# A diffusion backbone layer on one core: the vs projection by seven block products, stages reordered

## The chip, the cores and the metric

The kernel runs on one core of one Trainium2 chip. The metric is the device time of one execution in microseconds, lower is better. TensorE (PE) multiplies matrices, VectorE (DVE) and ScalarE (ACT) work elementwise, GpSimd (POOL) and SyncE (SP) here mainly issue DMAs; ACT issues a few as well.

## The reference

One layer with 512 latent tokens of width 1024 and 256 context tokens, all in float32. After a modulated RMS norm the input `hx` goes through one wide projection, and its parts feed two branches:

```python
z = h @ w_in
u, vs, q, r, ga, gb, k, v, lr = _split(z, IN_SPLITS)
a = _spatial_gating(gelu(u), gelu(vs), ...)     # u * (w_s . layer_norm(vs) + b_s), per chunk of 128 tokens
o, s_f, s_b = _gla_bidir(qh, k, v, lr, ...)      # gated linear attention, 4 heads, both directions
o = o * rsqrt(mean(o * o) + EPS)                 # per head
ob = o * gla_norm_g * silu(r)
merged = sigmoid(ga) * (a @ w_br_a) + sigmoid(gb) * (ob @ w_br_b)
x = x + g1x * (merged @ w_o)
```

Then a convolutional feed-forward (`ffn_w_up`, a 3x3 depthwise convolution, `ffn_w_down`) is added in the same way, and a final RMS norm gives the output. u, vs, r, ga and gb are each a product of 512 x 1024 by 1024 x 1024. The modulation vectors come from `c` through `w_ada`.

## The kernel before

**Float32 by three matmuls.** Every operand is split into a rounded high part and the residual, and a product is the sum of three matmuls (high x high, high x residual, residual x high) with 512 columns. A weight block of 512 KB (two or eight slices of 128 rows, 1024 numbers per partition) is loaded by SP (`stream_load`, line 237), cast by ACT (`wh`, line 249) and its residual made by DVE (`wl`, line 250). Five buffers each hold raw blocks, high parts and residuals. `specs` is the list of all blocks in the order of use; `weights()` takes the next one.

**Stages**, in order: first head's q, k, v; the other heads' k and q (`x_unit`), v of the last two heads (`v_units`); vs (`wide_tm`: four token tiles by two column halves, each 24 matmuls of line 408); u (eight units of 24 matmuls of line 390, channels first); r, ga, gb and the product with `w_br_a` (`gate`); the products with `w_br_b` and `w_o` (`wide_tm`); the feed-forward.

**Seven block products.** `gate` cuts a 1024 x 1024 product into two by two quadrants on either side and multiplies seven combinations instead of eight quadrants (the Strassen-Winograd scheme). Each of the seven has 24 matmuls (line 1360) and two weight blocks. The sums of quadrants of the input are made once (`hx_sum`, from a copy of `hx` in HBM, `fx_kept`). The sums of quadrants of the weights are made in HBM by POOL's DMAs: for each of two blocks of rows four copies, then four accumulating copies (`sums_build`, lines 214 and 216). A step of this is taken at each `weights()` call and at every second hook, and waits for the last matmul before it in the program; `SUMS0` and `DENSE` say where they start and where two are taken at once. For each gate ACT copies finished banks (`taken`) and DVE combines them (`combine`, line 1348).

**Hooks.** The attention of a head is a list of steps (transposes, scores, start state, states, decay of the next head, output); a hook between matmuls takes one step from the list. Before, the hooks in vs hold the third and fourth heads' attention. u's loop holds `sgu_part` (line 1252 and the two DVE instructions at 1254 and 1256), one unit late, which multiplies the normalised vs by the spatial weights and then by u; the result is written to HBM by POOL (`kept`). r's output goes through Silu and is multiplied by the attention output (`r_gate`); `ob_turn` (line 1336) transposes it and writes it to HBM during ga and gb.

**Background.** `ada2` builds the later modulation vectors on DVE (line 1216, one 256 KB load each), in steps called ticks: the list `ticks` says how many at each block of the gates. `behind_last` and `in_order` fix the order of such instructions on their engine. Otherwise a planner orders each engine's instructions when the program is built, by priority and its own costs. Two pools of 2 KB tiles, `heap` (43) and `late` (26), hold nearly everything; PSUM has four banks `mm` and four `gl`.

Of the kernel before, what the change touches and what calls it, by code (L numbers as in the profile page):

```python
# [16 lines left out]
P = 128  # L17
# [15 lines left out]
ENDS = 4  # L33
LEAD = 5
EARLY = 8
SUMS0 = 84
ADA2 = 7
DENSE = 10
SHSC = 6
# [5 lines left out]
def backbone_kernel(  # L45
# [27 lines left out]
    def late(shape, dt=F32, s="l"):  # L73
        return lp.tile(shape, dt, tag="l", name=nm(s))
# [69 lines left out]
    def w_cols(w, c0, n=P, k0=0, kn=KT):  # L144
        specs.append((w[k0 * P:(k0 + kn) * P, c0:c0 + n].rearrange("(k p) c -> p k c", p=P), kn, n))

    wi = w_in[0]
    for h in range(1, NH):
# [2 lines left out]
                w_cols(wi, O_V + 512, 512, 2 * k, 2)  # L151
        w_cols(wi, O_K + h * P)
        w_cols(wi, O_Q + h * P)
    for hf in range(2):
        for k in range(KT // 2):
            w_cols(wi, O_VS + hf * 512, 512, 2 * k, 2)
    for j in range(KT):
        w_cols(wi, O_U + j * P)
    R_AT = len(specs)
# [7 lines left out]
    def quarters(w, c0):  # L167
        return lambda b, row, col: w[(4 * b + 2 * row) * P:(4 * b + 2 * row + 2) * P,
                                     c0 + col * 512:c0 + (col + 1) * 512]

    def sum_tiles(blocks):
        return [[dp.tile([2 * P, 576], F32, name=nm("sum"))[:, :512] for _ in range(4)] for _ in range(blocks)]
# [6 lines left out]
        return ffn_w_down[0][r0:r0 + HALF[b] * P, col * 512:(col + 1) * 512]  # L179

    sums = [[dp.tile([n * P, 576], F32, name=nm("sum"))[:, :512] for _ in range(4)] for n in HALF]
    gate_weights = [(quarters(wi, c0), sum_tiles(2)) for c0 in (O_R, O_GA, O_GB)]
    gate_weights.append((quarters(w_br_a[0], 0), sum_tiles(2)))
    down_specs, specs = specs, []
    for g_quarter, g_sums in gate_weights:
# [81 lines left out]
    def weights():  # L267
        i = pos[2]
        pos[2] += 1
        for at, steps_ in building:  # L270
            for _ in range((i >= at) + (at <= i < DENSE)):
                next(steps_, None)
        stream_split(i + 2)
        stream_load(i + 1 + AHEAD)
        return splits.pop(i)
# [744 lines left out]

    def hook():
        hooked[0] += 1
        if hooked[0] % 2 and pos[2] < R_AT:
            next(building[1][1], None)
        if hooks:
            f = hooks.pop(0)
            f[0](*f[1:])
# [86 lines left out]
    o_tiles(1)  # L1114
    hooks += steps(1)
    v_units()
    ctx_k(3, x_unit(kxs, 3))
    x_unit(qxs, 3)
    o_tiles(2)
    hooks += steps(2)  # L1120
    o_tiles(3)
    hooks += steps(3)

# [2 lines left out]
    V.tensor_copy(ones_r, ones)  # L1126
    sw, swT, sgb = [], [], []

    def sgu_load():
        for i in range(2):  # L1130
            sw.append(late([P, 4, P], s="sw"))
            dma(sw[i], sgu_w[0, 4 * i:4 * i + 4].rearrange("g p q -> p g q"))
        for i in range(2):
            sgb.append(heap([P, 4, P], s="sgb"))
            dma(sgb[i], sgu_b[0:1, 4 * i:4 * i + 4, :].rearrange("o g p -> o (g p)").to_broadcast([P, 512]))

    def sgu_turn(i):
        ps = gl()
# [19 lines left out]
    vraw = [[None] * 4 for _ in range(2)]  # L1158
    stats = const([P, 4, 2, 6], "stats")

    behind = []

    def vs_done(hf, t, ps):
        vraw[hf][t] = (late if hf else heap)([P, 512], s="vr")
        A.activation(vraw[hf][t], ps, AF.Gelu)

        for h_, t_ in ((), ((), ((0, 0), (0, 1), (1, 0), (1, 1)), ((0, 2), (0, 3), (1, 2)), ((1, 3),))[t])[hf]:
            V.bn_stats(stats[:, t_, h_, :], vraw[h_][t_])
        if hf and t == 0:
            sgu_load()  # L1170
            behind.append(len(traced()))
        if hf and t == 1:
            in_order(behind.pop(), V.engine)

    wide_tm(hx, vs_done, hook)
    while hooks:
        hook()
    mv = const([P, 4, 2], "mv")
    for t in range(4):
        V.bn_aggr(mv[:, t, :], stats[:, t, :, :])  # L1180
    var = const([P, 5, 4], "var")
    V.tensor_scalar(var[:, 1:5, :], oss, 1.0 / 256, None, op0=ALU.mult)
    V.tensor_copy(var[:, 0, :], mv[:, :, 1])
    A.activation(var, var, AF.Sqrt, bias=eps_t, scale=1.0)
    V.reciprocal(var, var)
    vrs, ors = var[:, 0, :], var[:, 1:5, :]
    for hf in range(2):
        for t in range(4):
            z = vraw[hf][t]
            V.tensor_scalar(z, z, mv[:, t, 0:1], vrs[:, t:t + 1], op0=ALU.subtract, op1=ALU.mult)  # L1190


    bc_g = {}
# [45 lines left out]
                V.reduce_sum(cols[kind][:, j * 4:j * 4 + 4], t_, axis=AX.X)  # L1239
            yield  # L1240

    a_kept, ob_kept = [], {}
# [6 lines left out]
    def sgu_part(j, ug):  # L1249
        ps = gl()  # L1250
        for t in range(4):
            T.matmul(ps[:, t * P:(t + 1) * P], vraw[j // 4][t][:, (j % 4) * P:(j % 4 + 1) * P], swT[j // 4][:, j % 4, :], start=True, stop=True)  # L1252
        s_ = heap([P, 4, P], s="sg")
        V.scalar_tensor_tensor(s_, ps.rearrange("p (t r) -> p t r", t=4), lng[:, j:j + 1],
                               sgb[j // 4][:, j % 4, :].unsqueeze(1).to_broadcast([P, 4, P]), op0=ALU.mult, op1=ALU.add)
        V.tensor_tensor(ug, s_.rearrange("p t r -> p (t r)"), ug, op=ALU.mult)
        a_kept.append(spill(ug))

    hx_sums = {}

    def hx_sum(b):
        def quad(i, hf):
            t_ = heap([P, 2, 256], s="fq")
            for kk in range(2):
                dma(t_[:, kk], fx_kept[4 * b + 2 * i + kk][:, hf * 256:(hf + 1) * 256])
            return t_

        def kept(name, t_, p, q, op):
# [6 lines left out]
        a21, a22, a11, a12 = quad(0, 1), quad(1, 1), quad(0, 0), quad(1, 0)  # L1275
        kept("p1", a22, a21, a22, ALU.subtract)
        yield
        kept("s3", a21, a11, a21, ALU.subtract)
        yield
        kept("s2", a11, a22, a11, ALU.subtract)  # L1280
        yield
        kept("q4", a12, a12, a11, ALU.add)
        yield

    pieces = [z for z in (hx_sum(0), hx_sum(1)) for _ in range(4)]

    prev = None
    for j in range(KT):
        if j:
            next(pieces[j - 1])  # L1290
        w = weights()
        ps = mm()
        prod_cm(ps, w, hx)
        ug = heap([P, S], s="ug")
        A.activation(ug, ps, AF.Gelu)
        if j < 2:
            for i in range(2):
                (sgu_turn, sgu_bias)[j](i)
        if prev is not None:
            sgu_part(*prev)  # L1300
        prev = (j, ug)
    next(pieces[-1])
    sgu_part(*prev)


    ob_t = {}
# [10 lines left out]
    r_sum = of_sums(lambda name, b: hx_sums[name, b])  # L1317

    def r_silu(src):
        z = late([P, 512], s="obt")  # L1320
# [41 lines left out]

    banks = []

    def gate(out, pool, at={}, mids=late, quad=r_quad, sum_=r_sum):
# [24 lines left out]
        for t in range(2):  # L1390
            out(1, t + 2, combine(m5[t], X[t], ALU.subtract, pool))
        later(4)
        gate_product(Z, sum_("q4"))
        for t in range(2):
            out(1, t, combine(Z[t], u2[t], ALU.subtract, pool))
        later(5)
        gate_product(X, quad("a22"))
        later(6)
        for t in range(2):
            out(0, t + 2, X[t])  # L1400

    pending = []

    def r_out(hf, t, src):
# [3 lines left out]
        else:  # L1408
            pending.append((hf, t, z))

    bg += [ada2("g1"), ada2("sh", "sc", ahead=SHSC)]
    ticks = [0] * 2 + [1] * 6 + [0] * 6 + [0, 0] + [1] * 12 + [0, 1] * 7 + [1, 1, 2] * 5
    gate(r_out, heap, mids=heap)

    def squash(dst, name):
        def out(hf, t, src):
# [21 lines left out]

    sga, sgb_t = {}, {}
    def ga_step(i):  # L1440
        if i < 4:
            r_gate(*pending.pop(2 if i < 2 else 0))
        if i > 1:
            ob_turn(i - 2)

    gate(squash(sga, "sga"), heap, {i: lambda i=i: ga_step(i) for i in range(7)}, heap)
    found = {}

    def a_prep():
# [448 lines left out]
```

## Time and profile before

| | |
|---|---|
| median of 3 runs | 908.09 us (907.87 to 908.47) |
| profiled execution, span | 906.9 us |
| its own time, with what lies around the span as at the median | 906.9 + 1.2 = 908.1 us |
| PE busy | 892.4 us (98%), 4464 matmuls |
| DVE busy | 719.3 us (79%) |
| ACT busy | 468.7 us (52%) |
| POOL busy | 98.6 us (11%) |
| moved by DMA | 202.41 MB, mean 223 GB/s |
| queue of SP and ACT / queue of POOL | 137.39 MB, 47.1% / 61.04 MB, 30.4% of 16 engines |

The profile is of one execution. Times in it count from the span's start. L390 is line 390 of the kernel; in a group `mm<-hxh,wh` the tile written stands before the arrow. After the bar stand the busy time, the mean of one instruction in ns, and the idle time of the engine just before with what ended it. A matmul's own duration (390 ns) is longer than the distance from one to the next, as they are pipelined. A DMA share above 1 is possible, since it adds up the time of packets of several queues.

### The profile page before, as it was taken

The numbers are of one execution on the slowest core, as the hardware profiler recorded it, in microseconds if no ns is written. First come the engines' busy times: TensorE is split into PE (matmuls) and PEld (weight loads), VectorE is DVE, ScalarE is ACT, GpSimd is POOL, SyncE is SP. The second block draws the span as 40 slices with busy tenths as digits, with TensorE's granted clock in tenths as the row PEclk, the third lists the DMA queues.
The fourth block names the chain that finished last, engine by engine and source line by source line (L and its number), as shares of the span: only waits on it lengthen the run. The fifth ranks groups of instructions, "written<-read, shape, count | busy, mean of one in ns | idle before, by whom it ended". The sixth has DMA issues, their size and how long they took to land.

```text
span 906.9 us, 12500 instructions
## 1 busy us (share of the span) xinstructions
PE 892.4 (98%) x4464; PEld 744.0 (82%) x4464; DVE 719.3 (79%) x1205; ACT 468.7 (52%) x778; POOL 98.6 (11%) x154
## 2 busy tenths in 40 slices
PE   7999999999999999999999999999999999999996
PEld 5778888888888888888888889888888888888885
DVE  6468687869786478688998868897899987896996
ACT  6256455747533557678531448433343434356763
POOL 1311231212112200000000010001111110000000
PEclk9999999999999999999999999999999999999998
DMA  9985996899979999886999651998998893256552
GB/s 278 346 275 158 265 272 120 170 315 156 241 254 245 245 294 330 262 282 190 361 367 350 202 169 38 287 299 180 191 218 179 175 196 96 89 167 207 174 183 96
DMA packets 157291, 202.41 MB, mean 223 GB/s; under 512 B 9465, under 2 KB 88645, under 8 KB 157229
## 3 DMA queue, kind: packets, MB, share of 16 engines
q1 hardware_dynamic: 131229, 137.39, 47.1%
q0 software_dynamic: 24160, 61.04, 30.4%
q10 hardware_dynamic: 1840, 3.18, 0.9%
q8 instruction: 35, 0.57, 0.3%
q14 instruction: 27, 0.22, 0.1%
HBM read 193.19 MB, written 65.01 MB: 285 GB/s over the span
## 4 chain that ended last, share of the span: by engine, by line
PE 95%; DVE 1%; ACT 1%; DMA 1%; SPq 0%; issue 0%; ACTq 0%
PE mm L390 33%; PE mm L408 15%; PE mm L1360 12%; PE gl L1795 10%; PE gl L1360 5%; PE gl L926 3%; PE mm L690 2%; PE gl L408 2%; PE mm L1795 2%; PE gl L690 1%; PE mm L1038 1%; PE mm L1088 1%; PE gl L599 1%; PE gl L961 1%; PE gl L1252 1%; DMA wa<-in_w_ada_dram 1%
## 5 line engine op out<-in xcount | busy, mean ns | idle before, releaser
L249 ACT CAST wh<-raw 128x1024 fp32r<-128x1024 f32 x183 | 189.0, 1036 | 201.3 <-PE mm L390 104.0
L250 DVE TENSOR_TENSOR wl<-raw,wh 128x1024 fp32r<-128x1024 f32 x183 | 218.3, 1199 | 71.6 <-ACT wh L249 63.0
L390 PE MATMUL mm<-h2h,wh 128*128 128x512 f32 (+1 forms) x344 | 133.0, 387 | 0.0
L390 PE MATMUL mm<-h2l,wh 128*128 128x512 f32 (+1 forms) x344 | 133.0, 387 | 0.0
L390 PE MATMUL mm<-h2h,wl 128*128 128x512 f32 (+1 forms) x344 | 133.0, 387 | 0.0
L1647 DVE SCALAR_TENSOR_TENSOR cacc<-ca,ccol,cacc 128x441 f32<-128x441 f32 (+2 forms) x176 | 121.8, 694 | 4.4
L390 PEld LDWEIGHTS mm<-h2h,wl 128*128 128x128 f32 x344 | 64.6, 188 | 13.2
L390 PEld LDWEIGHTS mm<-h2l,wh 128*128 128x128 f32 x344 | 64.6, 188 | 13.1
L390 PEld LDWEIGHTS mm<-h2h,wh 128*128 128x128 f32 x344 | 64.6, 188 | 13.0
L1795 PE MATMUL gl<-wh,dah 128*128 128x512 f32 x132 | 51.3, 389 | 0.0
L1795 PE MATMUL gl<-wl,dah 128*128 128x512 f32 x132 | 51.3, 389 | 0.0
L1795 PE MATMUL gl<-wh,dal 128*128 128x512 f32 x132 | 51.3, 389 | 0.0
L1216 DVE SCALAR_TENSOR_TENSOR acc<-wa,cs,acc 128x512 f32<-128x512 f32 x64 | 45.8, 744 | 0.0
L1648 ACT ACTIVATE cacc<-cacc 128x512 f32<-128x512 f32 x22 | 13.9, 633 | 59.2 <-DVE cacc L1647 59.1
L214 POOL DMA_DIRECT2D sum<-in_ffn_w_down_dram x24 | 13.2, 554 | 281.6 <-PE mm L408 184.5
L390 PE MATMUL mm<-hxh,wh 128*128 128x512 f32 x104 | 41.3, 397 | 0.0
L390 PE MATMUL mm<-hxl,wh 128*128 128x512 f32 x104 | 40.6, 390 | 0.0
L390 PE MATMUL mm<-hxh,wl 128*128 128x512 f32 x104 | 40.5, 390 | 0.0
L216 POOL DMA_DIRECT2D sum<-sum x28 | 25.2, 899 | 113.1 <-PE mm L390 49.6
L408 PE MATMUL mm<-wh,hxh 128*128 128x512 f32 x88 | 34.7, 395 | 0.0
L408 PE MATMUL mm<-wl,hxh 128*128 128x512 f32 x88 | 34.4, 391 | 0.0
L408 PE MATMUL mm<-wh,hxl 128*128 128x512 f32 x88 | 34.3, 390 | 0.0
(464 smaller groups left out, 2031.4 us busy)
## 6 DMA issues: line engine op xcount, KB each, us to landing
raw<-sum SPq DMA_DIRECT2D x52, 512.0 KB, 4.4
wa<-in_w_ada_dram SPq DMA_DIRECT2D x96, 256.0 KB, 6.2
raw<-in_w_in_dram SPq DMA_DIRECT2D x46, 512.0 KB, 5.8
raw<-in_ffn_w_up_dram SPq DMA_DIRECT2D x44, 512.0 KB, 5.5
sum<-in_w_in_dram POOLq DMA_DIRECT2D x36, 512.0 KB, 7.7
sum<-in_ffn_w_down_dram POOLq DMA_DIRECT2D x30, 512.0 KB, 6.5
sum<-sum POOLq DMA_DIRECT2D x26, 512.0 KB, 7.4
raw<-in_ffn_w_down_dram SPq DMA_DIRECT2D x15, 512.0 KB, 4.2
```

The costliest lines, as they stand in the source:

```text
L216: G.dma_start(sums[b][dst], ap, accum_op=ALU.add)
L249: A.copy(wh, raw)
L250: V.tensor_tensor(wl, raw, wh.bitcast(F32), op=ALU.subtract)
L390: T.matmul(ps, a[:, k, :], b[:, c0:c0 + n], start=(k == 0 and i == 0), stop=(k == KT - 1 and i == 2))
L408: T.matmul(ps, a[:, t * P:(t + 1) * P], b[:, k % 2, :], start=(k == 0 and i == 0), stop=(k == KT - 1 and i == 2))
L690: T.matmul(fps[i], a, b, start=(k == 0 and z == 0), stop=(k == KT - 1 and z == 2))
L926: T.matmul(ps, p_, q_, start=(start and z == 0), stop=(stop and z == 2))
L1216: behind_last(lambda: V.scalar_tensor_tensor(acc[i], coming.pop(0), cs[:, k, 0:1], acc[i], op0=ALU.mult, op1=ALU.add), V)
L1360: T.matmul(banks[t], a(kk, t), w[:, kk, :], start=(first and b == 0 and kk == 0 and i == 0), stop=(b == 1 and kk == 1 and i == 2), skip_gr ...
L1647: V.scalar_tensor_tensor(o, a_[:, r0 + dy:r1 + dy, c0 + dx:c1 + dx], wcol(tap), o, op0=ALU.mult, op1=ALU.add)
L1648: A.activation(acc, acc, AF.Gelu)
L1795: T.matmul(ps, a, w[:, kk, :], start=(first and kk == 0 and i == 0), stop=(last and kk == n_ - 1 and i == 2), skip_group_check=True)
```

## The change

- The order becomes u, r, vs, ga, gb. vs goes through `gate` and has its own quadrant sums in HBM, so `specs` has 14 blocks for vs behind r in place of 8 ahead of u, and `SUMS0` moves from 84 to 90. Five gates' sums (80 steps) are built in place of four (64).
- Sum steps are taken at every hook from the eighth block on, and from r on at two of three blocks.
- The third head's attention is put on the hook list ahead of k and q of the fourth; the rest of it and the fourth head's runs in u, with two hooks in each unit.
- u's Gelu is taken later than its matmuls (up to three units wait in PSUM), the results stay in SBUF until ga.
- `hx_sum` is spread over u and the first two products of r; the last sum ("q4") is written over the upper-right quadrant of `hx`, which no gate reads.
- r's outputs are multiplied by the attention in r and vs, `ob_turn` runs in vs and ga, the spatial weights are loaded in r and turned in vs, and `sgu_part` runs in ga, two after each of four products, with its results written to HBM on ACT's queue.
- The ticks are spread anew: five in r, seven in vs, as before from ga on.

```diff
-SUMS0 = 84
+SUMS0 = 90
...
-    for hf in range(2):
-        for k in range(KT // 2):
-            w_cols(wi, O_VS + hf * 512, 512, 2 * k, 2)
...
-    gate_weights = [(quarters(wi, c0), sum_tiles(2)) for c0 in (O_R, O_GA, O_GB)]
+    gate_weights = [(quarters(wi, c0), sum_tiles(2)) for c0 in (O_R, O_VS, O_GA, O_GB)]
...
-            for _ in range((i >= at) + (at <= i < DENSE)):
+            for _ in range((i >= at and not (at == 1 and i >= R_AT and i % 3 == 0)) + (at <= i < DENSE)):
                 next(steps_, None)
...
-        if hooked[0] % 2 and pos[2] < R_AT:
+        if (hooked[0] % 2 or pos[2] >= 8) and pos[2] < R_AT:
             next(building[1][1], None)
...
     v_units()
+    o_tiles(2)
+    hooks += steps(2)
     ctx_k(3, x_unit(kxs, 3))
     x_unit(qxs, 3)
-    o_tiles(2)
-    hooks += steps(2)
     o_tiles(3)
     hooks += steps(3)
...
-    wide_tm(hx, vs_done, hook)
-    while hooks:
-        hook()
...
-        a_kept.append(spill(ug))
+        spills.append((j, ug))
...
     for j in range(KT):
-        if j:
-            next(pieces[j - 1])
         w = weights()
-        ps = mm()
-        prod_cm(ps, w, hx)
...
+        ups.append(mm())
+        for k in range(KT):
+            prod_k(ups[-1], w, hx, k, 0, S)
+            if k == 3:
+                hook()
+                for _ in range((0, 0, 1, 1, 1, 2, 1, 1)[j]):
+                    u_out()
+        hook()
+        if j == 2:
+            piece()
+        if j == 7:
+            piece()
+    u_out()
+    while hooks:
+        hook()
+    piece()
...
+    def r_step(i):
+        if i < 2:
+            piece()
+        if i in (3, 5):
+            sgu_load(i // 2 - 1)
+
+    bg += [ada2("g1", ahead=5), ada2("sh", "sc", ahead=SHSC)]
+    ticks = [0] * 4 + [1, 0] * 5 + [1, 0] * 7 + [0, 0] + [1] * 12 + [0, 1] * 7 + [1, 1, 2] * 5
+    gate(r_out, heap, {i: lambda i=i: r_step(i) for i in range(7)}, heap)
...
+    def vs_out(hf, t, src):
+        z = vraw[hf][t] = heap([P, 512], s="vr") if not hf else src
+        A.activation(z, src, AF.Gelu)
+        V.bn_stats(stats[:, t, hf, :], z)
+
+    def vs_step(i):
+        if i < 4:
+            r_gate(*pending.pop(2 if i < 2 else 0))
+        if i in (1, 2):
+            sgu_turn(i - 1)
+        if i in (3, 5):
+            sgu_bias(i // 2 - 1)
+        if i > 0:
+            ob_turn(i - 1)
...
+    gate(vs_out, heap, {i: lambda i=i: vs_step(i) for i in range(7)}, late, pool1=late)
...
+    def sgu_step(i):
+        while spills:
+            j, ug = spills.pop(0)
+            a_kept[j] = spill(ug, adma)
+        for n in ((), (0, 1), (2, 3), (4, 5), (6, 7), (), ())[i]:
+            sgu_part(SGU_ORDER[n])
...
     def ga_step(i):
-        if i < 4:
-            r_gate(*pending.pop(2 if i < 2 else 0))
-        if i > 1:
-            ob_turn(i - 2)
+        if i < 2:
+            ob_turn(i + 6)
+        sgu_step(i)
...
     def gb_step(i):
-        if i < 3:
-            ob_turn(i + 5)
         a_step((4, 2, 2, 2, 2, 2, 2)[i])
```

More of the change, by code (lines that the diff above doesn't have):

```diff
@@ L1127, in backbone_kernel, with sgu_load @@
     sw, swT, sgb = [], [], []
[L1129 to L1135, printed above, removed]
+    def sgu_load(i):
+        sw.append(late([P, 4, P], s="sw"))
+        dma(sw[i], sgu_w[0, 4 * i:4 * i + 4].rearrange("g p q -> p g q"))
+        sgb.append(heap([P, 4, P], s="sgb"))
+        dma(sgb[i], sgu_b[0:1, 4 * i:4 * i + 4, :].rearrange("o g p -> o (g p)").to_broadcast([P, 512]))
     def sgu_turn(i):
@@ L1154, in sgu_bias @@
                                    lnb[:, 4 * i + g:4 * i + g + 1], sgb[i][:, g, :], op0=ALU.mult, op1=ALU.add)
[L1158 to L1173, printed above, removed]
-    wide_tm(hx, vs_done, hook)
-    while hooks:
-        hook()
[L1178 to L1190, printed above, removed]
     bc_g = {}
@@ L1240, in ada2 @@
             yield
-    a_kept, ob_kept = [], {}
+    a_kept, ob_kept = {}, {}
     def spill(src, start=G.dma_start):
@@ L1247, in spill, with sgu_part @@
         return d
-    def sgu_part(j, ug):
+    ugs, spills = [], []
+    def sgu_part(j):
+        ug = ugs[j]
         ps = gl()
@@ L1273, in kept @@
             hx_sums[name, b] = pair
-        a21, a22, a11, a12 = quad(0, 1), quad(1, 1), quad(0, 0), quad(1, 0)
+        a21, a22, a11 = quad(0, 1), quad(1, 1), quad(0, 0)
+        yield
         kept("p1", a22, a21, a22, ALU.subtract)
+        yield
+        kept("s2", a22, a22, a11, ALU.subtract)
+        a12 = quad(1, 0)
         yield
@@ L1279, in hx_sum, with piece, u_out @@
         yield
-        kept("s2", a11, a22, a11, ALU.subtract)
-        yield
[L1282 to L1287, printed above, removed]
+        V.tensor_tensor(a12, a12, a22, op=ALU.add)
+        for kk in range(2):
+            hi, lo = (z[:, 256:512] for z in hx[4 * b + kk])
+            A.copy(hi, a12[:, kk])
+            V.tensor_tensor(lo, a12[:, kk], hi.bitcast(F32), op=ALU.subtract)
+        yield
+    sums_of = [hx_sum(0), hx_sum(1)]
+    def piece():
+        behind_last(lambda: [next(z) for z in sums_of], V)
+    ups = []
+    def u_out():
+        ug = heap([P, S], s="ug")
+        A.activation(ug, ups.pop(0), AF.Gelu)
+        ugs.append(ug)
     for j in range(KT):
-        if j:
-            next(pieces[j - 1])
         w = weights()
-        ps = mm()
-        prod_cm(ps, w, hx)
[L1294 to L1303, printed above, removed]
+        ups.append(mm())
[14 more added lines that the diff above has]
+    piece()
     ob_t = {}
@@ L1315, in r_quad, with r_sum @@
                    for z in range(2)]
-    r_sum = of_sums(lambda name, b: hx_sums[name, b])
+    x_sum = of_sums(lambda name, b: hx_sums[name, b])
+    def r_sum(name):
+        return r_quad("a12") if name == "q4" else x_sum(name)
     def r_silu(src):
@@ L1363, in backbone_kernel, with gate @@
     banks = []
-    def gate(out, pool, at={}, mids=late, quad=r_quad, sum_=r_sum):
+    def gate(out, pool, at={}, mids=late, quad=r_quad, sum_=r_sum, pool1=None):
+        pool1 = pool1 or pool
         fresh = not banks
@@ L1390, in gate @@
         for t in range(2):
-            out(1, t + 2, combine(m5[t], X[t], ALU.subtract, pool))
+            out(1, t + 2, combine(m5[t], X[t], ALU.subtract, pool1))
         later(4)
@@ L1394, in gate @@
         for t in range(2):
-            out(1, t, combine(Z[t], u2[t], ALU.subtract, pool))
+            out(1, t, combine(Z[t], u2[t], ALU.subtract, pool1))
         later(5)
@@ L1400, in gate @@
             out(0, t + 2, X[t])
+    orv = const([P, 4, 4], "orv")
+    V.tensor_scalar(orv, oss, 1.0 / 256, None, op0=ALU.mult)
+    A.activation(orv, orv, AF.Sqrt, bias=eps_t, scale=1.0)
+    V.reciprocal(orv, orv)
+    ors = orv
     pending = []
@@ L1409, in r_out @@
             pending.append((hf, t, z))
-    bg += [ada2("g1"), ada2("sh", "sc", ahead=SHSC)]
-    ticks = [0] * 2 + [1] * 6 + [0] * 6 + [0, 0] + [1] * 12 + [0, 1] * 7 + [1, 1, 2] * 5
-    gate(r_out, heap, mids=heap)
+    def r_step(i):
[6 more added lines that the diff above has]
+    gate(r_out, heap, {i: lambda i=i: r_step(i) for i in range(7)}, heap)
+    vraw = [[None] * 4 for _ in range(2)]
+    stats = const([P, 4, 2, 6], "stats")
+    def vs_out(hf, t, src):
[11 more added lines that the diff above has]
+            ob_turn(i - 1)
+    SGU_ORDER = (4, 5, 6, 7, 0, 1, 2, 3)
+    gate(vs_out, heap, {i: lambda i=i: vs_step(i) for i in range(7)}, late, pool1=late)
+    mv = const([P, 4, 2], "mv")
+    for t in range(4):
+        V.bn_aggr(mv[:, t, :], stats[:, t, :, :])
+    var = const([P, 4], "var")
+    A.activation(var, mv[:, :, 1], AF.Sqrt, bias=eps_t, scale=1.0)
+    V.reciprocal(var, var)
+    for hf in (1, 0):
+        for t in range(4):
+            z = vraw[hf][t]
+            V.tensor_scalar(z, z, mv[:, t, 0:1], var[:, t:t + 1], op0=ALU.subtract, op1=ALU.mult)
+    def sgu_step(i):
[4 more added lines that the diff above has]
+            sgu_part(SGU_ORDER[n])
     def squash(dst, name):
@@ L1440, in ga_step @@
     def ga_step(i):
-        if i < 4:
-            r_gate(*pending.pop(2 if i < 2 else 0))
-        if i > 1:
-            ob_turn(i - 2)
-    gate(squash(sga, "sga"), heap, {i: lambda i=i: ga_step(i) for i in range(7)}, heap)
+        if i < 2:
+            ob_turn(i + 6)
+        sgu_step(i)
+    gate(squash(sga, "sga"), heap, {i: lambda i=i: ga_step(i) for i in range(7)}, late)
     found = {}
```

## The prediction

> **What bounds the kernel now.** I read the page's busy shares and chain first, then the chain in order of time, to cut the middle of the span into stages.
>
> ```profile
> span 906.9 us, 12500 instructions
> PE 95%; DVE 1%; ACT 1%; DMA 1%; SPq 0%; issue 0%; ACTq 0%
> ```
>
> ```profile
> 180.87 2.72 PE mm L408 x12
> ...
> 230.26 5.47 PE mm L408 x24
> 235.73 1.43 PE gl L926 x12
> 237.16 5.47 PE mm L408 x24
> 242.63 4.31 PE gl L926 x36
> 246.94 5.47 PE mm L390 x24
> 252.41 0.87 PE gl L1140 x8
> 253.28 5.46 PE mm L390 x24
> 258.75 0.94 PE gl L1151 x4
> 259.68 0.89 PE gl L1252 x8
> ...
> 299.58 5.46 PE mm L1360 x24
> 305.03 5.44 PE gl L1360 x24
> 310.47 16.32 PE mm L1360 x72
> 326.79 5.44 PE gl L1360 x24
> 332.23 10.88 PE mm L1360 x48
> ...
> 354.00 0.44 PE gl L1336 x4
> ```
>
> Each piece starts where the one before ends. So vs runs from 180.87 to 246.94 with attention (L926) between its matmuls, u to 299.58 with the spatial gate (L1252) between, then r, then ga. The windows by stage (busy time of PE, PEld, DVE, ACT, POOL; clock; DMA share; GB/s) say the same:
>
> ```profile
> 160.00:246.90 86.90, 86.90 (x502) 76.50 (x501) 69.94 (x153) 53.14 (x111) 16.79 (x23) 1.00 0.91 224
> 246.90:299.60 52.70, 52.70 (x270) 44.83 (x269) 36.81 (x61) 21.36 (x34) 8.93 (x14) 1.00 0.85 244
> 299.60:337.70 38.10, 38.10 (x169) 31.54 (x169) 23.51 (x31) 21.04 (x27) 5.68 (x7) 1.00 1.01 280
> 337.70:378.00 40.30, 40.30 (x189) 33.29 (x187) 31.75 (x41) 27.61 (x37) 0.00 (x0) 1.00 0.89 300
> 440.00:460.00 20.00, 20.00 (x90) 16.57 (x89) 20.00 (x28) 10.64 (x14) 0.00 (x0) 1.00 1.05 406
> ```
>
> PE is busy all the time at full clock, so each matmul taken out is time won, as long as nothing else makes PE wait. What is nearly full beside it is the DMA engines: in r their share is 1.01.
>
> **Term 1, matmuls.** vs is eight output tiles of 24 matmuls (8 blocks of the contraction, 3 terms), 192. Seven block products have 24 each, 168. The 24 that go are one piece of r: 38.10/168 = 0.227 us each, **-5.44 us**. Bounds: 5.44 to 5.47 by the pieces. Every other PE instruction is moved, not added: spatial gate 8 x 0.89, its transposes and bias 0.87 + 0.94, head outputs 8 x 0.44.
>
> **Term 2, splits and sums on ACT and DVE in vs.** Blocks go from 8 to 14, so 6 more casts and residuals; four combinations, four copies of a bank and two from bank to bank come in. Rows of ga, which has the same form:
>
> ```profile
> L250 DVE TENSOR_TENSOR wl<-raw,wh 128x1024 fp32r<-128x1024 f32 x16 | 19.5, 1221 | 8.5 <-ACT wh L249 8.5
> L1216 DVE SCALAR_TENSOR_TENSOR acc<-wa,cs,acc 128x512 f32<-128x512 f32 x12 | 9.0, 746 | 0.0
> L1348 DVE TENSOR_TENSOR dc<-gl,dt 128x512 f32<-128x512 f32 x3 | 2.0, 682 | 0.0
> L1328 DVE SCALAR_TENSOR_TENSOR obt<-o,var,obt 128x256 f32<-128x256 f32 x8 | 3.3, 477 | 0.0
> ```
>
> vs will last 38.1 + 0.87 + 0.94 + 6 x 0.44 = 42.6 us on PE. DVE in it: 14 x 1.22 + 4 x 0.68 + four head tiles 3.3 + eight statistics at about 0.7 + spatial bias and transposes about 5 + 7 modulation steps x 0.75 = 39 us. It fits at 91%; price 0, covered by PE's 42.6. Between 0 and one late bank (0.7 us).
>
> **Term 3, the spatial gate in ga.** It brings eight pairs of DVE instructions and the normalisation:
>
> ```profile
> L1254 DVE SCALAR_TENSOR_TENSOR sg<-gl,vec_b,sgb 128x512 f32<-128x512 f32 x6 | 4.5, 744 | 0.0
> L1256 DVE TENSOR_TENSOR ug<-sg,ug 128x512 f32<-128x512 f32 x6 | 4.1, 686 | 0.0
> L1190 DVE TENSOR_SCALAR vr<-vr,mv,var 128x512 f32<-128x512 f32 x8 | 3.7, 538 | 0.0
> ```
>
> ga on PE becomes 38.1 + 8 x 0.89 + 2 x 0.44 = 46.1 us. DVE: 31.75 - 3.3 (head tiles, gone to vs) + 8 x 1.43 + 3.7 + last statistics about 2 = 45.6 us. DVE is full there, but what is queued includes 12 modulation steps (9.0 us) that nobody waits for soon. The first gate matmul comes after ga's second product, 10.9 us in; the chain to it (Gelu, statistics, root with a table load, half of the normalisation) is about 6 us. I take 0; bounds 0 to 5.4 (DVE late by one product).
>
> **Term 4, attention earlier.** Three hooks of the third head move behind the units of k and q of the fourth; the other 13 go into u's 16 slots. The slots are half a product apart (2.72 us) as in vs now, and the Gelus of u are held back until after the last decay's Exp. Up to three of four banks hold unread u. Price 0; the matmuls between cover it as the first windows row shows (86.90 of 86.90 busy with the same steps). Bounds 0 to 1.
>
> **Term 5, DMAs.** 16 more steps on POOL's queue (8 copies, 8 accumulations), 6 more blocks on SP's. The eight spills of the gate move from POOL to ACT's queue, in ga; each is issued a product after the DVE instruction that it waits for, so the casts queued behind it on ACT should not stand. No sum is late: counted in the code, r's 16 are asked for before v as now, vs's 16 during v, ga's by u's second unit, gb's by u's end, br_a's 16 over r and the first five products of vs, and each is read a stage or more later. What matters is crowding. Prices, as time of all engines, from three windows (gate copies; mostly accumulations; loads alone), and POOL's queue in r now:
>
> ```profile
> q0 software_dynamic: 873, 3.18, 60.7%
> ```
>
> ```profile
> q0 software_dynamic: 2200, 4.30, 77.2%
> ```
>
> ```profile
> q1 hardware_dynamic: 4337, 8.10, 105.0%
> ```
>
> ```profile
> 299.88 0.91 POOL L216 DMA_DIRECT2D sum<-in_w_br_a_dram  x1 [3.60 <-PE gl L1252]
> ...
> 319.30 0.87 POOL L216 DMA_DIRECT2D sum<-sum  x1 [5.00 <-DMA sum<-sum]
> ```
>
> Of 17, 32 and 20 us, per 512 KB: copy 1.7 us, accumulation 3.0, load 1.36. r now: 14 x 1.36 + 6 half loads x 0.68 + 5 x 3.0 + two spills 1.4 = 39.5 of 38.1 (1.04; the row says 1.01). r then: 19.0 + 5 x 0.68 + 8 x 1.7 + 3.0 + spatial weights 2.7 + last quadrants 1.4 = 43.1 of 38.1. vs then: 19.0 + 7 x 0.68 + 6 spills x 0.68 + 7 x 3.0 = 48.9 of 42.6. Taking the 1.05 of the loads row as full, 3.1 and 4.2 us are too much, 7.3 together. That is made up by POOL's queue (its sums have tens of us to spare) or by the weights' lead. The lead in r now:
>
> ```profile
> 304.80 1.22 DVE L250 TENSOR_TENSOR wl<-raw,wh 128x1024 fp32r<-128x1024 f32 x1 [1.64 <-ACT wh L249]
> ```
>
> ```profile
> 320.21 1.05 ACT L249 CAST wh<-raw 128x1024 fp32r<-128x1024 f32 x1 [3.67 <-DMA raw<-in_w_in_dram]
> ...
> 329.70 2.51 DVE L250 TENSOR_TENSOR wl<-raw,wh 128x1024 fp32r<-128x1024 f32 x2 [2.04 <-ACT wh L249]
> ```
>
> Five buffers: the residual done at 306.0 is used at 312.1, 6 us ahead; the pair done at 331.0 and 332.2 is used from 332.5 and 333.8, 1.5 us ahead. So ACT already waits for loads in r, and five accumulations cost 4.5 us of lead without reaching PE. Bounds of what PE will wait: 0 (POOL takes it) to 7.3 (all on the loads, no lead left). I take 0.5, near the low end, because the row it is nearest to, r now, wrote nothing on PE, and because the accumulations wait for each other and spread.
>
> **Term 6, the rest.** One more table load and root on ACT (some 1.6 us of an engine with 9 to 17 us free per stage); six more modulation steps before ga and fewer behind br_a, where PE has no idle time to win. 0.
>
> **The sum.** 906.9 + 1.2 around it (median 908.09 less the span) - 5.44 + 0.5 = **903.2 us**.
>
> **Rivals.**
> *Loads late.* While an accumulation is under way, SP's share falls:
>
> ```profile
> q0 software_dynamic: 281, 0.54, 84.8%
> q1 hardware_dynamic: 114, 0.23, 20.5%
> ```
>
> These 4 us (from 304) moved 0.23 MB of loads where r's PE uses 0.77. If packets alternate, a load moves one block while an accumulation does (1.36 + 3.0 = 4.4 us, in which PE uses 0.84 MB): 0.32 MB or 1.6 us lost each, 13 us for eight, of which about 7 come back in the gaps: 6, about the whole lead. With what r has already taken (3.1 us), PE waits about 3: 906.2; up to 7.3: 910. For it: the row, and ACT's 3.67. Against: the chain of sums throttles itself (5.00 above).
> The Trainium skill, DMA: Bandwidth & Descriptors, Queues, rings and completion order, says the engines take turns between queues packet by packet; the row's 20.5 to 84.8 is nearer to one in four than to the one in two of time that equal packets would give, so the trace agrees only in direction. The same page's Specifications give about 358 GB/s of HBM per core; by it a block would cost 1.46 us (an estimate), the excess in term 5 would be 10.1, and the upper bound of the wait with it. The 406 GB/s row is above that, and the measurement decides.
> *DVE sets ga's pace (slower).* If the two free banks of the gate's parts are freed late, each of four pairs holds PE for one residual, one modulation step and one combination, 1.22 + 0.75 + 0.68 = 2.65, 10.6 in all: 903.2 + 10.6 = 913.8. It decides once the waits pass 5.44 + 1.8. For it: 45.6 of 46.1. Against: 20.00 of 20.00 DVE from 440 to 460 with PE fully busy.
> *Nothing is won.* The steps moved into u or the heap's slots hold PE as long as vs gets shorter: 908.1. Against: no idle PE anywhere around them now.
>
> **Chances.** Forecast (902.2 to 904.2) 0.57; loads late 0.24, of which 0.16 still faster by over 0.2% and 0.08 within; nothing won 0.06; slower 0.13. 0.2% is 1.8 us, about what a measurement here can tell from no change. Faster 0.73, same 0.14, slower 0.13. The range 902.0 to 908.8 leaves out the slow case and the end of the second.
>
> **What would show it.** Right: the vs pieces are seven of 24 matmuls, the span is near 902.0, PE full in the windows of r, vs, ga. Loads late: PE gaps in r or vs released by DVE wl or ACT wh, and these by DMA raw. DVE in ga: gaps before L1252 matmuls released by DVE. Wrong altogether: gaps in u.

## The result and the profile after

The changed kernel takes **918.35 us** at the median (915.42 to 921.61, 4 runs), beside 908.19 us (907.87 to 908.47) of the kernel before in the same comparison: a ratio of 1.0112, 95% interval 1.0087 to 1.0137. It is 10 us slower where 5 us faster was forecast. The profiled execution is the longest of the four, 921.61 us with a span of 919.9; the accounts below are made against the span of before, 906.9.

The page of after (busy shares, then the two DMA queues, then the shares of the chain that ended last):

```profile
span 919.9 us, 12530 instructions
PE 892.9 (97%) x4440; PEld 741.5 (81%) x4440; DVE 728.1 (79%) x1217; ACT 480.4 (52%) x795; POOL 105.4 (11%) x162
...
q1 hardware_dynamic: 132861, 140.53, 47.5%
q0 software_dynamic: 26848, 67.34, 32.5%
...
PE 81%; DMA 9%; DVE 4%; ACT 3%; SPq 2%; issue 1%; ACTq 0%; DVEq 0%
```

The 24 matmuls are gone (4464 to 4440), and yet PE's busy time has not fallen. Of the chain 9% is DMA now, where it was 1%. POOL's queue moves 67.34 MB, where it moved 61.04.

Windows of after (columns: busy time and instructions of PE, PEld, DVE, ACT, POOL; granted clock; DMA share; GB/s): the first 60 us, the next 500, and then u, r, vs and ga alone.

```profile
0.00:60.00 60.00, 51.97 (x386) 38.75 (x387) 33.78 (x101) 27.08 (x62) 13.43 (x34) 1.00 1.00 317
60.00:560.00 500.00, 488.67 (x2449) 409.13 (x2448) 384.42 (x656) 280.10 (x480) 65.64 (x94) 0.99 0.90 264
...
199.90:254.10 54.20, 52.00 (x282) 44.83 (x281) 35.94 (x80) 32.06 (x68) 13.42 (x19) 0.97 1.04 263
254.10:292.60 38.50, 38.13 (x167) 30.99 (x166) 28.91 (x41) 24.05 (x36) 5.93 (x10) 1.00 1.01 335
292.60:345.70 53.10, 45.22 (x204) 36.95 (x203) 36.04 (x54) 29.21 (x39) 6.18 (x7) 0.90 1.07 302
345.70:392.60 46.90, 46.90 (x246) 39.97 (x245) 41.33 (x59) 27.95 (x37) 0.00 (x0) 1.00 0.79 255
```

vs lasts 53.10 us, not 42.6, and PE is idle for 7.88 of them; u loses 2.2 the same way. r loses 0.4 and ga nothing. The granted clock, 1.00 in every row of before, is 0.90 in vs and 0.97 in u. PE's waits in 60 to 560 us (sum, times, longest):

```profile
PE gl L1135 <- DVE swT L1137: 5.7, 1, 5.7
PE gl L1319 <- ACT obf L1321: 2.1, 1, 2.1
PE gl L923 <- ACT st L967: 1.9, 1, 1.9
```

None of the three releasers is the cause. They are a copy of the spatial weights, a turned output of r and a state of the attention, each short. The first two stood in their engine's queue behind an instruction that waited for a load; the third waited for sums on DVE that had stood behind one. DVE around the first wait, ACT around the first two, and the chain of waits (start, duration):

```profile
310.00 1.22 DVE L247 TENSOR_TENSOR wl<-raw,wh 128x1024 fp32r<-128x1024 f32 x1 [4.80 <-ACT wh L246]
314.06 1.23 DVE L247 TENSOR_TENSOR wl<-raw,wh 128x1024 fp32r<-128x1024 f32 x1 [2.84 <-ACT wh L246]
315.21 0.68 DVE L1137 COPY swT<-gl 128x512 f32<-128x512 f32 x1
```

```profile
308.92 1.05 ACT L246 CAST wh<-raw 128x1024 fp32r<-128x1024 f32 x1 [5.15 <-DMA raw<-in_w_in_dram]
...
317.52 1.04 ACT L246 CAST wh<-raw 128x1024 fp32r<-128x1024 f32 x1 [3.01 <-DMA raw<-sum]
318.48 0.68 ACT L1321 ACTIVATE obf<-gl,vec_b 128x512 f32<-128x512 f32 x1
```

```profile
215.52 12.53 DMA fq<-fx
228.16 0.69 DVE fq L1232
...
288.72 13.44 DMA raw<-sum
302.23 15.27 DMA raw<-sum
```

In vs the chain is two weight loads of 13 to 15 us, one after the other; the page's median for that load is 4.6. In u it is a 12.5 us load of a quadrant half (`fq`), for which DVE waited 5.67 us until 228.16 while the attention's splits and state updates stood behind it. What shared the DMA engines with the loads in vs is on POOL (L213 is the accumulating copy of the sums; in brackets the idle time before and what ended it):

```profile
287.87 0.91 POOL L213 DMA_DIRECT2D sum<-in_w_br_a_dram  x1 [4.34 <-PE gl L1343]
293.31 0.89 POOL L213 DMA_DIRECT2D sum<-in_w_br_a_dram  x1 [4.53 <-PE mm L1343]
299.20 1.77 POOL L213 DMA_DIRECT2D sum<-in_w_br_a_dram  x2 [5.01 <-PE mm L1343]
305.06 0.87 POOL L213 DMA_DIRECT2D sum<-sum  x1 [4.08 <-PE gl L1319]
```

Five accumulations of `w_br_a`'s sums go out within 17.2 us, and PE stops at 310.2.

**The account** of the span, 13.0 us longer: 24 matmuls fewer, -5.4; idle PE between 60 and 560 us, 11.33 beside 0.35 in before, +11.0; matmuls at a lower clock, +4.9 (busy time in vs 45.22 where 42.30 are needed, in u 52.00 where 50.0 are, by a version below without gaps); a later start of this execution, +1.4 (PE busy 53.41 us of the first 60 in before, 51.97 here; over the profiled executions of all versions below it is 51.5 to 53.7, in either order of the stages). That is 11.9; 1.1 is not assigned.

### The profile page after: what moved, and what is told of

Read it like the earlier page. It is cut to its first block, busy times and chain, and to the rows that moved or that the text cites. A ratio compares the mean times of both kernels' runs of the same rounds, so it can differ in the third digit from the quotient of the medians.

```text
span 919.9 us, 12530 instructions
## 1 busy us (share of the span) xinstructions
PE 892.9 (97%) x4440; PEld 741.5 (81%) x4440; DVE 728.1 (79%) x1217; ACT 480.4 (52%) x795; POOL 105.4 (11%) x162
## 3 DMA queue, kind: packets, MB, share of 16 engines
q0 software_dynamic: 26848, 67.34, 32.5%
## 4 chain that ended last, share of the span: by engine, by line
PE 81%; DMA 9%; DVE 4%; ACT 3%; SPq 2%; issue 1%; ACTq 0%; DVEq 0%
PE mm L387 30%; PE mm L1343 11%; PE mm L405 10%; PE gl L1824 10%; DMA raw<-sum 4%; PE gl L1343 4%; DMA fq<-fx 2%; PE gl L923 2%; PE mm L1824 2%; SPq L297 1%; PE mm L687 1%; DMA wa<-in_w_ada_dram 1%; PE mm L1035 1%; PE mm L1085 1%; PE gl L405 1%
## 5 line engine op out<-in xcount | busy, mean ns | idle before, releaser
L246 ACT CAST wh<-raw 128x1024 fp32r<-128x1024 f32 x189 | 194.8, 1036 | 191.7 <-PE mm L387 86.5
L247 DVE TENSOR_TENSOR wl<-raw,wh 128x1024 fp32r<-128x1024 f32 x189 | 225.9, 1201 | 66.1 <-ACT wh L246 65.9
L213 POOL DMA_DIRECT2D sum<-sum x32 | 27.9, 873 | 141.5 <-PE mm L387 56.9
L1343 PE MATMUL mm<-wh,xs 128*128 128x512 f32 x128 | 41.1, 392 | 0.0
L1343 PE MATMUL mm<-wl,hxh 128*128 128x512 f32 x96 | 38.1, 397 | 0.4 <-DVE wl L247 0.4
L1343 PE MATMUL mm<-wh,hxh 128*128 128x512 f32 x96 | 38.4, 400 | 0.0
```

The costliest lines, as they stand in the source:

```text
L213: G.dma_start(sums[b][dst], ap, accum_op=ALU.add)
L246: A.copy(wh, raw)
L247: V.tensor_tensor(wl, raw, wh.bitcast(F32), op=ALU.subtract)
L1343: T.matmul(banks[t], a(kk, t), w[:, kk, :], start=(first and b == 0 and kk == 0 and i == 0), stop=(b == 1 and kk == 1 and i == 2), skip_gr ...
```

## The experiments

The theory after the result: accumulating DMAs take the engines from the loads that PE's operands wait for, and how close together they stand decides. Rivals: the stages' new order itself, the attention's depth in u, plain traffic whatever its kind.

**1. Every accumulation of the sums a plain copy of the same bytes** (kernel after; the sums are not formed):

```diff
-                        G.dma_start(sums[b][dst], ap, accum_op=ALU.add)
+                        G.dma_start(sums[b][dst], ap)
```

> The changed kernel with every accumulating step made a plain copy of the same 512 KB, so the sums of weights are not formed (that part of the computation is left out); number, order and waits of the DMAs are as they were. Crowding: loads land early, no idle PE in vs or u, 902 to 905 us, that is, the 5.4 us of the matmuls come out. Order: 915 to 920, as the order of all engines is the same.

904.38 us (903.35 to 905.29), 0.9955 of before [0.9938, 0.9971]. Its waits, and its page's queue:

```profile
PE gl L941 <- ACT junk L1010: 0.5, 1, 0.5
PE gl L923 <- DVE mx L875: 0.3, 1, 0.3
```

```profile
q0 software_dynamic: 18912, 67.34, 22.5%
```

No gap above 0.5 us is left, with order, bytes and issues unchanged. It gains 3.9 us on before (908.24 in this comparison), of the 5.4 of the matmuls. So the order, the splits, the attention in u and the spatial gate in ga cost some 1.5 us at most, all together; the accumulations cost 14 us. The same 67.34 MB took 32.5% of 919.9 us in after and 22.5% of 903.6 here, 299 and 203 us; of the 128 transfers of 512 KB half were accumulations, so one costs 96/64 = 1.5 us of all engines more than a copy.

**2. Only the fourth gate's (`w_br_a`'s) eight accumulations as copies** (its sums are not formed):

```diff
-                        G.dma_start(sums[b][dst], ap, accum_op=ALU.add)
+                        G.dma_start(sums[b][dst], ap, **({} if sums is gate_weights[4][1] else dict(accum_op=ALU.add)))
```

> The kernel after, with the eight accumulations of the fourth gate's weight alone (those that run from r's seventh product to vs's fifth) written as plain copies of the same bytes; the sums of that weight are left out of the computation so, and gate values of the fourth branch differ. Theory: vs's gap of about 9 us and its slow matmuls go, as u's (2 us, whose accumulations are of another weight) stays: 906 to 909 us. Rival (vs's gap comes from the copies and loads together, whatever the accumulation): vs's gap stays above 5 us and the time above 914.

907.95 us (905.53 to 910.12), 1.0003 of before [0.9993, 1.0014]. Eight DMAs are worth some 10 us. The queues in the 25 us from the first of these eight on, in after (287 to 312) and then here (286 to 311):

```profile
q0 software_dynamic: 1365, 3.01, 55.3%
q1 hardware_dynamic: 2867, 4.65, 52.9%
```

```profile
q1 hardware_dynamic: 3904, 6.70, 70.9%
q0 software_dynamic: 935, 3.38, 33.2%
```

As copies POOL's queue moved more in less time, and SP's loads got 6.70 MB through where they got 4.65. What in an accumulation holds the engines longer, no run separates. vs has no gap here. u's stays (1.9 and 1.0 us), as expected, and r has one of 1.9.

**3. The eight accumulations (and their copies) moved from r and vs to ga and gb:**

```diff
-            for _ in range((i >= at and not (at == 1 and i >= R_AT and i % 3 == 0)) + (at <= i < DENSE)):
+            for _ in range((i >= at and not (at == 1 and R_AT <= i < R_AT + 28)) + (at <= i < DENSE)):
```

> The changed kernel with the 16 steps of the sums for w_br_a taken in ga and gb (one at each weight block) and none in r and vs. Theory (crowding: weight loads land late in vs because accumulating steps on POOL's queue hold the DMA engines): the 8 us of idle PE in vs and the slow clock behind it go, the 2 us in u stay: 906 to 910 us. Rival (order: the waits in vs are made by the order of ACT's and DVE's work there, the DMAs only look late): 915 to 920, the gap at the turned spatial weights stays.

918.25 us (916.89 to 918.9), 1.0106 [1.0087, 1.0125]: the gap moved with them. vs runs through, and gb waits instead, 6.2 us near 400 us for a cast behind a load; the chain of waits:

```profile
377.32 15.42 DMA raw<-in_w_in_dram
392.76 8.22 DMA aq<-kept
```

The expected 906 to 910 was missed. ga's lower DMA share in after (0.79) was not room enough: the first four two at a time, the eight accumulations from 361 to 393 us are as dense as in vs.

**4. Hooks taken as in before (one part undone):**

```diff
-        if (hooked[0] % 2 or pos[2] >= 8) and pos[2] < R_AT:
+        if hooked[0] % 2 and pos[2] < R_AT:
```

> The kernel after with one part undone: each second hook of the attention takes a sum step throughout, as in before, instead of each hook from the eighth weight block on. Fewer steps stand in u and so more of them behind it. Theory: u's gap (2 us) shrinks or goes, and the third and fourth gate's steps that are pushed into r and vs keep a gap there or make it larger: 912 to 925 us. Rival (the denser hooks alone made the loss): 902 to 907 us.

921.57 us (920.79 to 922.38), 1.0146 [1.0131, 1.0161]. u's gap goes (PE busy 20.00 of 20.00 us from 220 to 240), vs keeps a gap of 7.8 us between 300 and 320, and the sums that are pushed back make new ones from 400 on. Density in the hooks is not the loss; too many sums in too little time are, wherever one packs them.

**5. The kernel before with vs's 16 sums built as well**, read by nobody:

```diff
+    gate_weights.insert(1, (quarters(wi, O_VS), sum_tiles(2)))
...
-    for g_quarter, g_sums in gate_weights:
+    for g_quarter, g_sums in gate_weights[:1] + gate_weights[2:]:
```

> The kernel before with the quadrant sums of vs's weights built as well, behind r's, and not used: 16 more steps on POOL's queue in the old order of stages. Crowding: the steps that stand behind them move into r and ga, where blocks are used every 2.7 us, and PE waits there: 910 to 915. Order: nothing waits for the extra steps, 908.

928.83 us (927.77 to 929.61), 1.0223 [1.0208, 1.0239]: the old order with the new sums loses 20.6 us, far more than the 2 to 7 expected. The chain of waits shows three loads, one behind the other:

```profile
314.30 18.46 DMA raw<-sum
...
335.20 18.64 DMA raw<-sum
...
357.35 20.19 DMA raw<-sum
```

The kernel after is 10.5 us faster than this, and 5.4 of these are its matmuls. So the change's order and its sparser sums behind u take back some 5 of the 20.6 us (an estimate: the two also differ in the number of blocks that vs loads).

**6. u's wait.** First the second of u's late pieces (`piece`, whose sums read the `fq` loads) behind the last hook:

```diff
-        if j == 7:
-            piece()
     u_out()
...
     piece()
+    piece()
```

> The changed kernel with the second step of hx_sum (p1) behind the last hook of u and not at its last unit. Crowding: the quadrants still land late (12 us), but DVE no longer stands on them ahead of the attention's instructions, so the 2 us gap in u goes, with the slow clock behind it some 3 us; vs keeps its 8 us: 912 to 917. Rival (the attention's own chain of ACT and DVE makes the gap in u): gap and time stay, 915 to 920.

921.45 us (917.6 to 922.69), 1.0136 [1.011, 1.0162], and u's gap as before (1.8 us). The edit did not move what it was to move: the planner still put that DVE sum at 227.38 us, where it waited 5.37 us for its load. Then both pieces tied by an order without a semaphore to the attention's last copy on DVE (`last_o` holds the names of these copies, filled where each is made):

```diff
-        if j == 7:
-            piece()
...
-    piece()
+    anchor = next(z for z in reversed(traced()) if z.engine == V.engine and z.name in last_o)
+    for _ in range(2):
+        start = len(traced())
+        piece()
+        first = next(z for z in traced()[start:] if z.engine == V.engine)
+        tc.add_manual_dep(first, anchor.name, mybir.DependencyInfo(
+            mybir.DependencyClass.NoSync, mybir.DependencyReason.DATA), reason="after_o")
```

> The kernel after, but u's two late pieces of the first branch's load (the quadrant halves that VectorE sums at the end of u) stand, by an order without a semaphore, behind the attention's last copy on VectorE, so that VectorE no longer sits in front of that copy waiting for a load. Theory (accumulating DMAs crowd the other transfers, and whatever waits for these in an engine's queue blocks what stands behind): u's idle of about 2 us near 237 us and the slow matmuls after it go, vs's gap of about 9 us near 315 us stays: 914 to 917 us. Rival (u's gap is the attention's own depth, not the load): the gap stays where it is and the time stays at 917 to 919. Second rival: the sums come later and hold up r: a new gap of over 2 us between 240 and 290 us.

918.2 us (917.75 to 918.87), 1.0119 [1.0103, 1.0134]:

```profile
PE gl L1325 <- ACT obf L1327: 5.5, 1, 5.5
PE mm L1349 <- DVE wl L247: 3.4, 1, 3.4
PE gl L1137 <- DVE swT L1139: 1.5, 1, 1.5
```

u's gap is gone, so it was the queue behind one waiting sum and not the attention's depth. But the time stays: r now waits 3.4 us, as the second rival said. While the loads behind are late, a wait taken from one queue comes out at the next.

**7. The same sums, spread.** Eight sum steps are taken in the first branch's key product, near 62 to 75 us, where before's DMA share is 0.28 and 0.24 in two 10 us windows, and from r on one block in four takes a step:

```diff
-            for _ in range((i >= at and not (at == 1 and i >= R_AT and i % 3 == 0)) + (at <= i < DENSE)):
+            for _ in range((i >= at and not (at == 1 and i >= R_AT and i % 4 != 1)) + (at <= i < DENSE)):
...
         prod_k(kps, k1, hx, k, 0, S)
+        next(building[1][1])
```

> The kernel after with the same sums of weights, spread otherwise: eight sum steps (a copy or an accumulation each) are taken one per key product of the first branch, near 62 to 75 us, where before's DMA engines stand idle, and from r on one block in four takes a step instead of two in three, so the fourth gate's eight accumulations are spread over r, vs and ga. Theory: not the amount of accumulation but how close together it stands beside the weight loads sets vs's gap: the gap falls from about 9 us to under 2, u's stays or shrinks: 905 to 912 us. Rival (the accumulations cost the loads the same wherever they stand between 60 and 400 us): gaps of the same sum turn up elsewhere and the time stays at 915 to 920.

907.79 us (906.85 to 909.82), 1.0006 [0.9996, 1.0015]: every accumulation is there, and vs runs without a wait. u's gap stays (1.9 and 0.6). With the tie of the second edit under 6 as well:

> The two edits together: eight sum steps near 62 to 75 us, one block in four from r on, and the two late pieces of u behind the attention's last copy. Theory: both gaps go, and what is left is the 24 matmuls fewer (5.4 us less than before's 908.2) plus a remainder: 903 to 906 us, faster than both kernels. Rival (the crowding costs the same wherever it stands): 912 to 918.

**904.37 us** (902.91 to 906.14), **0.996 [0.9946, 0.9974]**: faster than both kernels. Its windows of r, vs and ga, and POOL's accumulations in vs:

```profile
249.90:288.00 38.10, 38.10 (x170) 31.55 (x169) 32.31 (x47) 28.13 (x41) 2.67 (x3) 1.00 0.96 287
288.00:330.30 42.30, 42.30 (x202) 35.07 (x202) 33.73 (x51) 27.17 (x36) 3.52 (x4) 1.00 1.01 320
330.30:376.80 46.50, 46.50 (x243) 39.62 (x242) 41.13 (x58) 27.79 (x37) 0.89 (x1) 1.00 0.84 265
```

```profile
288.29 0.88 POOL L213 DMA_DIRECT2D sum<-in_w_br_a_dram  x1 [9.54 <-PE mm L1350]
300.05 0.87 POOL L213 DMA_DIRECT2D sum<-sum  x1 [10.88 <-PE gl L1326]
312.75 0.88 POOL L213 DMA_DIRECT2D sum<-sum  x1 [11.83 <-PE gl L1326]
```

Accumulations some 12 us apart leave PE full in all three stages at full clock; between 60 and 560 us it idles 0.86 us in all.

**8. Each half of the spreading alone**, both with the tie. Without the early steps, and a step at every second block from r on:

```diff
-            for _ in range((i >= at and not (at == 1 and i >= R_AT and i % 3 == 0)) + (at <= i < DENSE)):
+            for _ in range((i >= at and not (at == 1 and i >= R_AT and i % 2 == 0)) + (at <= i < DENSE)):
```

> The version that beat both kernels, without its eight early steps near 62 to 75 us: u's late pieces stay tied, and from r on one block in two takes a sum step (not two in three), so the fourth gate's eight accumulations run over vs and the start of ga. Theory (u and r need the early steps, since the third and fourth gate's steps are otherwise all packed into u; spacing alone only moves the crowding): gaps of 3 to 10 us in sum stay in r, vs or ga, 908 to 917 us. Rival (the spacing behind u is what counts): no gap over 1 us, 903 to 906 us.

915.65 us (911.66 to 916.9), 1.0066 [1.0043, 1.009], with 4.3 and 4.8 us of waits in r and in ga, there behind its second product. With the early steps and after's density (`i % 3 == 0`):

> The version that beat both kernels, with its eight early steps and tied pieces, but at the density of the kernel after from r on (two blocks in three), so the fourth gate's eight accumulations all stand in r's first six products. Theory (accumulations close together beside the weight loads starve them): a gap of 3 to 10 us in r or at the start of vs, 907 to 915 us. Rival (the stock of loads carries r, since eight steps fewer stand in u): no gap over 1 us, 903 to 906 us.

913.21 us (912.23 to 914.5), 1.0055 [1.004, 1.007]. POOL in it, and the window that follows:

```profile
247.27 0.91 POOL L213 DMA_DIRECT2D sum<-in_w_br_a_dram  x1 [4.34 <-PE mm L387]
...
258.60 1.77 POOL L213 DMA_DIRECT2D sum<-in_w_br_a_dram  x2 [5.01 <-PE gl L1350]
263.58 0.87 POOL L213 DMA_DIRECT2D sum<-sum  x1 [3.20 <-PE mm L1350]
```

```profile
260.00:280.00 20.00, 12.71 (x47) 9.96 (x46) 11.27 (x18) 11.30 (x19) 2.12 (x3) 0.83 0.96 248
```

It is the same picture as vs in after, 41 us earlier and in another stage: five accumulations within 16.3 us, then a PE gap of 7.3 us. This pair differs from the second version of run 7 in the spacing alone: accumulations 10 to 13 us apart in place of 6 us or less are worth some 9 us. The early steps were not tested so cleanly. Without them 16 steps are left when r begins, and one block in four would give 14 up to the end of gb (56 blocks, counted in the code); so the first run here is denser as well, and how much of its loss is owed to the missing early steps stays open. Neither half did it alone as tested.

**9. Control: the early steps in the kernel before:**

```diff
         prod_k(kps, k1, hx, k, 0, S)
+        next(building[1][1])
```

> The kernel before, with eight sum steps taken one per key product of the first branch, near 62 to 75 us, and otherwise as it was. Control for the version that beat both kernels: before has no gap that earlier sums could close, so 906.5 to 908.5 us, within 0.2% of before; if the early steps alone won time, under 905.

908.35 us (906.78 to 909.06), 0.9997 [0.9987, 1.0006]. Earlier sums alone win nothing; the gain of the last version under 7 is the change's own, with its crowding taken out.

## Why the prediction was wrong

**Term 1 was right in PE's work, and only in part in time.** In the version without gaps and with all its sums PE is busy for 887.5 us, 4.9 below before's 892.4. Its span is 2.5 us below before's, in an execution that starts 1.9 us later (PE busy 51.51 of the first 60 us) and idles 0.5 more: -5.4 + 1.9 + 0.5 = -3.0, with 0.5 left over. By medians it gains 3.1 us on before (904.37 beside 907.50, interval 2.4 to 4.9); the whole 5.4 was measured in no run. That 904.37 lies near the forecast 903.2 does not bear the forecast out, as it is another version.

**Terms 2 and 3 were right, with their stage lengths.** vs was put at 42.6 and ga at 46.1; without gaps they take 42.3 and 46.5. DVE in ga was overestimated (45.6; 41.3 in after), so the rival that DVE sets ga's pace had less for it than it was given.

**Term 4 failed**: bounds 0 to 1, measured 2.2 us of idle PE and 2.0 of slow matmuls in u. The attention itself fits, as run 1 and the second version of run 7 show. What was not budgeted is u's own DMAs: term 5 added up r and vs alone, while the DMA share in u came to 1.04. And the DVE sum that waited for the `fq` load was not asked who stands behind it; run 7 with and without the tie differs by 3.4 us.

**Term 5 is the step that failed most**: taken at 0.5 with bounds 0 to 7.3; r and vs lost 0.4 and 10.5 us (38.5 of 38.1, 53.1 of 42.6). Its prices were good: 3.0 for an accumulation beside 1.7 for a copy, where run 1 gives 1.5 between them. The summing was wrong. It spread the excess over a whole stage and let POOL's queue take it up, "because the accumulations wait for each other and spread". The row that it leaned on, r of before, holds mostly the sums of sums (`sum<-sum`), and two of its five steps are released by a DMA. In the burst in vs four of the five are taken from `w_br_a`, which wait for no other accumulation, and PE released every step: POOL issued at PE's pace and did not give way.

By the same prices (an estimate, made after the result) the burst itself is short: 17.2 us of PE's pace are 6.3 blocks of 1.36 us, 8.6, and five accumulations 15.0, together 23.6 us in 17.2 x 1.05 = 18.1: 5.5 us too much, against a lead of 1.5 to 6. At one accumulation in 11 us, four blocks, it is 5.5 + 3.0 = 8.5 of 11.6. A budget over the burst tells these two versions apart, where the one over the stage did not.

Density alone is no threshold, though. Before's own r takes its five accumulations within 19.4 us (299.88 to 319.30), by the same working 4.3 us too much, and PE does not wait. The DMA share ahead of that burst was 0.85 (u of before); ahead of the one in vs it was 1.04 and 1.01 (u and r of after). So what is left of the lead when a burst begins should count too; no run changes that alone.

**The rival "loads late" had the mechanism**, its rows too (DVE `wl` and ACT `wh` late by DMA `raw`), but not the size, 906.2 to 910. It credited 7 us that "come back in the gaps"; in the 25 us under run 2 the two queues together hold 108% of the engines' time, which leaves no gaps. It also left out what stands behind a late cast: the copy that frees a `gl` bank (L1137), and that of a turned output of r (L1321), by which the wait came out at instructions that need no weight.

**The slow clock was in no term.** The prediction priced a wait at its length. After a gap PE worked at a lower clock, 4.9 us in all, nearly half of what the idle time cost.

"Wrong altogether: gaps in u" was the sign named, and it was there.

## What to carry to other kernels

Where DMAs build operands beside the loads, budget them over each burst, of a length that the lead in buffers can cover, and not over the stage; count the lead that is left when it begins; put the expensive ones where the queue's windows are empty and keep them apart. A price per transfer is not enough when what paces the transfers is the engine that they starve. For each instruction that may wait for a load, ask what stands behind it in its engine's queue, and count a PE gap for more than its length.

## What the runs showed of the hardware

**The clock after a gap.** PE in after around its longest waits (groups of matmuls, start and duration; those not yet up to speed, then those at full speed):

```profile
315.94 1.12 PE L1135 MATMUL gl<-ident,sw 128*128 128x128 f32 x4 [5.73 <-DVE swT L1137]
319.21 1.12 PE L1319 MATMUL gl<-ident,obt 128*128 128x128 f32 x4 [2.15 <-ACT obf L1321]
...
321.83 0.63 PE L1343 MATMUL mm<-wl,hxh 128*128 128x512 f32 x1
322.26 0.63 PE L1343 MATMUL mm<-wh,hxl 128*128 128x512 f32 x1
...
323.69 0.39 PE L1343 MATMUL mm<-wl,hxh 128*128 128x512 f32 x1
323.91 0.39 PE L1343 MATMUL mm<-wh,hxl 128*128 128x512 f32 x1
```

Matmuls start 0.43 us apart until 322.7 and 0.22 to 0.24 from 323.0 on; the granted clock is 0.50 from 315 to 320. The Trainium skill, TensorE: Matmul & The Clock Gate, Part 1, says the array runs at half clock after an idle window of about 3.4 us and recovers after a busy one, with 512-column matmuls 426.7 ns apart at half clock: the spacing agrees with the trace to the last digit shown. A shorter gap sufficed here: u's of 1.87 us was followed by a granted clock of 0.75 from 235 to 240, and one of 1.88 us in the first version of run 7 by 0.66. In run 2 gaps of 1.9 us in u and in r left it at 1.00. So a short gap may or may not cost this; on what it depends, these runs don't settle.

**A load beside accumulations**: those of sums in the chains of waits took 13 to 20 us where the median of such loads is 4.6 and 4.7 on the pages of after and of run 5, with SP's queue in after still at half of the engines' time. The Trainium skill, DMA: Bandwidth & Descriptors, Queues, rings and completion order, says the engines take turns between queues by packets; the trace agrees in direction only: in the 25 us under run 2 both queues hold about as much of the engines' time (53 and 55%), but the profile counts 2867 packets of SP's queue beside 1365 of POOL's.

Open are 1.1 us of after's longer span and the cause of the later start.
